# FFN 2 of a hybrid encoder layer: feature tiles 2 and 3 move from single units to a 2x2 pair, and the norms' small steps are reordered

## The chip, the cores and the metric

The kernel runs on one core of a Trainium2 chip. The metric is the device time of one execution in microseconds (us). The engines are named as in the profile: PE (TensorE, the matmuls; PEld are its weight loads), DVE (VectorE), ACT (ScalarE), POOL (GpSimd), SP (SyncE, which issues the loads).

## The reference

One layer on 512 tokens of width 1024 in float32: a half-step SwiGLU FFN, a mixer with two branches (a gated linear recurrence and a windowed attention), their gated sum through `w_o`, and a second half-step FFN. Each is wrapped in RMS norms.

```python
h = h + 0.5 * rms_norm(swiglu(rms_norm(h, ffn1_pre_g), ffn1_w1, ffn1_w3, ffn1_w2), ffn1_post_g)
u = rms_norm(h, mix_pre_g)
...
y_b = swa_sink_attention(q, k, v, attn_sinks, bias) @ w_attn_out
merged = g[:, :, 0] * y_a + g[:, :, 1] * y_b
h = h + rms_norm(merged @ w_o, mix_post_g)
f = swiglu(rms_norm(h, ffn2_pre_g), ffn2_w1, ffn2_w3, ffn2_w2)
h = h + 0.5 * rms_norm(f, ffn2_post_g)
```

`swiglu(x, w1, w3, w2)` is `(silu(x @ w1) * (x @ w3)) @ w2` with an inner width of 2816, which is 22 feature tiles of 128.

## The kernel before

**Number format.** Each float32 operand of a matmul is split in two: ACT copies it to a rounded `hi`, DVE subtracts to get `lo` (`split2`, L186; for weights `split_to`, L146 to L160). A product is three matmuls: hi by hi, lo by hi, hi by lo. The normalized and transposed input of an FFN lies in `uT` (hi and lo, 8 k-tiles of 128 x 512 tokens).

**A unit** (`unit`, `mm_feat`, L194 to L211) is one feature tile of one weight: 8 k-tiles x 3 = 24 matmuls of 128 x 512. In mid-stream it calls `point` twice; `later(n, fn)` (L170) puts a step on a hand-planned list that falls due n points on. So the order of work on ACT, DVE and POOL beside the matmuls is written out by hand.

**A pair** (`Pairs`, L460 to L582) takes two feature tiles of one weight as a 2x2 block product with seven multiplications in place of eight. A job is seven products (`mm_s`, L447) of 4 k-tiles x 3 matmuls of 128 x 256. Its right-hand operands are three quarters of `uT` (`b11`, `b21`, `b22`) and T1 to T4, sums of the quarters (`sums`, L729), which have to be split as well (`to_slots`, L738; `to_uT`, into `uT` itself, L743). Its left-hand operands are quarters of the two raw weight tiles and their sums S1 to S4: `prep(m, 0)` adds them on POOL (L500 to L503), `prep(m, 1)` to `prep(m, 4)` split the raw tile, S1/S2, S3/S4 and the last quarter on ACT and DVE (L191, L192). `run` makes the next job's `prep` 1 to 4 and the sums of the one behind it beside each job. The product with T4 of a job is issued behind the next job's second product (`last`). ACT evicts the first product of a job at L532.

**FFN 2 before** is tiles 0 and 1 as units inside w_o's function, tiles 2 and 3 as four units (`swiglu_units("w1b", "w3b", 2, NC2, hid)`, NC2 = 4), then nine pairs (18 jobs), then the product with w2.

**Around it.** The eight w_attn_out units (`for i in range(8)` behind `mg_out`, L1120 to L1135) come first; then w_o in `tok_gemm` (L314 to L401): for the first two k-tiles all token blocks, then four token blocks one after the other, each followed by its norms, with PE turning the result by transposes (L294). At its end the `first` list of four weights (tiles 0 and 1 of w1 and w3) is multiplied with token columns 0 to 255, and after the last transposes with columns 256 to 511. The T sums and the first job's weights are made beside these last halves and beside tiles 2 and 3.

**The norms.** `post_norm` (L253 to L268) takes two halves of 512 columns from PSUM: ACT squares and sums one (`junk`), DVE multiplies it with the gain (`fg`). `rstd2` (L227 to L235) then makes one over the root in five steps: `b` (DVE) from the first half's sum, the root `r` (ACT) from the second half's sum with `b` as bias, `v`, `e` and `r2` (DVE). DVE adds the result to `h` (L266). `norms` (L270 to L286) follows with the next norm's squares and products (`hg`, L278) and a second `rstd2`. The last token block of FFN 2 calls `post_norm` with three parts and stores each.

**Memory and queues.** All large tiles share 42 slots of 128 x 1024 float32 (NSLOT); a load is issued when a slot is free and in the fixed sequence `order`, on SP's queue. Matmul results use 8 PSUM banks. Each engine works in order.

Of the kernel before, what the change touches and what calls it, by code (L numbers as in the profile page):

```python
# [51 lines left out]
def hybrid_layer(ctx: ExitStack, tc: tile.TileContext, a: dict, out: bass.AP):  # L52
# [171 lines left out]

    NEWT = -0.5 * D**0.5

    def rstd2(ss):  # L227

        b, v, r, e, r2 = (small(1, x) for x in ("b", "v", "r", "e", "r2"))
        dve.tensor_scalar(out=b, in0=ss[:, 0:1], scalar1=D * EPS, scalar2=None, op0=ALU.add)  # L230
        act.activation(r, ss[:, 1:2], AF.Abs_reciprocal_sqrt, bias=b)
        dve.tensor_scalar(out=v, in0=ss[:, 1:2], scalar1=b, scalar2=None, op0=ALU.add)
        dve.tensor_scalar(out=e, in0=r, scalar1=v, scalar2=r, op0=ALU.mult, op1=ALU.mult)
        dve.tensor_scalar(out=r2, in0=e, scalar1=-3.0, scalar2=r, op0=ALU.add, op1=ALU.mult)
        return r2  # L235

    def rstd4(s4):

# [11 lines left out]
        pool.dma_start(out=t, in_=bass.AP(tensor=src.tensor, offset=src.offset, ap=[[0, P], [1, D]]))  # L250
        return t

    def post_norm(acc, t, gpost, scale, dst, after=None, parts=()):  # L253

        ss = small(2, "ss")
        fg = slot([P, D], name="fg")
        junk = slot([P, D], name="junk")
        cs = [slice(n * 512, (n + 1) * 512) for n in range(2)]
        for n, c in enumerate(cs):
            act.activation(junk[:, c], acc[n], AF.Square, accum_out=ss[:, n : n + 1])  # L260
            dve.scalar_tensor_tensor(out=fg[:, c], in0=acc[n], scalar=scale * NEWT, in1=gpost[:, c], op0=ALU.mult, op1=ALU.mult)
        r = rstd2(ss)
        if len(parts) > 2:
            cs = parts
        for n, c in enumerate(cs):
            dve.scalar_tensor_tensor(out=dst[:, c], in0=fg[:, c], scalar=r, in1=h[t][:, c], op0=ALU.mult, op1=ALU.add)  # L266
            if after:
                after(n, c)  # L268

    def norms(acc, t, gpost, scale, gpre, spill):  # L270

        hg = slot([P, D], name="hg")
        junk = slot([P, D], name="junk")
        ss = small(2, "ss")

        def half(n, c):
            act.activation(junk[:, c], h[t][:, c], AF.Square, accum_out=ss[:, n : n + 1])
            dve.scalar_tensor_tensor(out=hg[:, c], in0=h[t][:, c], scalar=NEWT, in1=gpre[:, c], op0=ALU.mult, op1=ALU.mult)  # L278

        post_norm(acc, t, gpost, scale, h[t], half)  # L280
        if spill:
            sp.dma_start(out=h_scr[t], in_=h.pop(t))
        r = rstd2(ss)
        dve.tensor_scalar(out=hg[:, :512], in0=hg[:, :512], scalar1=r, scalar2=None, op0=ALU.mult)
        act.activation(hg[:, 512:], hg[:, 512:], AF.Copy, scale=r)
        return hg  # L286
# [24 lines left out]
            act.activation(xf[half, t // 2][:, :, (t % 2) * P : (t % 2 + 1) * P], v, AF.Copy)  # L311


    def tok_gemm(nm, xs, n, R, gpost_name, scale, gpre_name, first, x_to=None, xf=None, spill=False):  # L314

# [37 lines left out]
        for t in range(NT):  # L355
            for ns in ((0,), (1,)):
                for k in range(F, n):
                    mm_tok(accs(t), xs[k], t, w[k], k == 0, k == n - 1, ns)
            if not gpre_name:
                o = slot([P, D], name="o")  # L360

                def store(nn, c, t=t, o=o):
                    sp.dma_start(out=out[t * P : (t + 1) * P, c], in_=o[:, c])

                last = (slice(0, 512), slice(512, 768), slice(768, D)) if t == NT - 1 else ()
                post_norm(acc[t], t, gpost, scale, o, store, last)
                continue
            if t == NT - 1:
                break
            if t >= 1:  # L370
                trs[t - 1] = transpose_mm(us[t - 1])
            if t == NT - 2:

                transpose_out(trs[t - 1], t - 1)
            us[t] = norms(acc[t], t, gpost, scale, gpre, spill)
            if t == NT - 2 and xf:
                transpose_xf(trs[t - 1], t - 1, xf)
            elif t == 1:
                transpose_out(trs[t - 1], t - 1, xf)
# [4 lines left out]
        for i, key in enumerate(first):  # L384
            ws.append(get(*key, ahead=len(first) - 1 - i, rawahead=2))
            bs.append(bank("f"))
            if i == len(first) - 1:
                trs[t] = transpose_mm(us[t])
                transpose_out(trs[t], t)
                if xf:  # L390
                    transpose_xf(trs[t - 1], t - 1, xf)
                    transpose_xf(trs[t], t, xf)
            mm_feat(bs[i], ws[i], 0, 256)
            if i == 0:
                trs[t - 1] = transpose_mm(us[t - 1])
                us[t] = norms(acc[t], t, gpost, scale, gpre, spill)
                transpose_out(trs[t - 1], t - 1)
# [62 lines left out]
    class Pairs:  # L460
# [13 lines left out]
        def prep(self, m, i, eng=None):  # L474
# [41 lines left out]
        def run(self, tail, hooks={}):
# [604 lines left out]
    def mg_out(i, ps):  # L1121
# [5 lines left out]
        dve.scalar_tensor_tensor(out=m[:, 1, :], in0=t, scalar=0.5, in1=f32(m[:, 0, :]), op0=ALU.mult, op1=ALU.subtract)  # L1127
        mg.append(m)

    for i in range(8):  # L1130
        if i:
            w = get("wao", i)
        ps = bank("f")
        mm_feat(ps, w, xh=xh, xl=xl)
        later(1, lambda i=i, ps=ps: mg_out(i, ps))  # L1135
    del xh, xl, OH, OL, KS, QS, BT
    h_load([h_scr[t] for t in range(NT)])
    xf = {(hh, th): slot([P, 4, 256], name="xf") for hh in range(2) for th in range(2)}
    bs = tok_gemm("wo", mg, KT, RO, "mix_post_g", 1.0, "ffn2_pre_g", [("w1b", 0), ("w3b", 0), ("w1b", 1), ("w3b", 1)], xf=xf)


    hid = Hidden()
    X2, tn = {"b11": uview(0, 0), "b21": uview(1, 0), "b22": uview(1, 1)}, []
    later(1, lambda: hid.f.append(silu_mul(bs[0], bs[1])))
    later(2, lambda: hid.f.append(silu_mul(bs[2], bs[3])))
    later(1, lambda: tn.extend(sums(xf)))
    later(2, lambda: xf.clear())
    for i in range(3):
        later(2 + i, lambda i=i: X2.update({f"t{i + 1}": to_slots(tn[i])}))
    pairs_b = Pairs("w1b", "w3b", NC2, X2, hid)  # L1150
    end = 2 * 2 * (NC2 - 2)
    for i, at_ in enumerate((end - 7, end - 4, end - 3, end - 2, end - 1)):
        later(at_, lambda i=i: pairs_b.prep(0, i))
    later(end, lambda: pairs_b.prep(1, 0))
    swiglu_units("w1b", "w3b", 2, NC2, hid)
    point(True)
    X2["t4"] = to_uT(tn[3], 0, 1)
    tn.clear()
    pairs_b.run(w2_ahead)
    X2 = pairs_b = None  # L1160
    tok_gemm("w2b", hid, FT, RF, "ffn2_post_g", 0.5, None, [], hid.to)

# [12 lines left out]
RO = 6  # L1175

NC1 = 6
NC2 = 4


# [52 lines left out]
```

## Time and profile before

| what | value |
|---|---|
| median of 3 runs | 1137.44 us (1137.4 to 1137.97) |
| profiled execution | 1138.07 us |
| its span in the profile | 1136.3 us |
| granted TensorE clock | 0.999 |
| w_attn_out units, first to last matmul | 692.2 to 735.4 us of the span |
| w_o with its norms | 735.5 to 781.4 us |
| tiles 0 and 1, then tiles 2 and 3 as units | 781.4 to 806.1, 806.1 to 827.9 us |
| nine pairs | from 827.9 us |

Instruction rows in what follows give the start in us, the duration, the engine, the line, the operation, output <- inputs, shapes, how many are merged, and in brackets how long the engine was idle before and what released it. Rows of grouped instructions give busy us, mean ns of one, and the idle time before them with its releasers.

### The profile page before, as it was taken

Reading aid. Unit: us, or ns where it says so; the run is one execution under the profiler, and the core shown is the slowest. Engines: PE = TensorE matmul, PEld = TensorE weight load, DVE = VectorE, ACT = ScalarE, POOL = GpSimd, SP = SyncE. Lnnn points to the kernel's source line nnn. Section 1 sums busy time; section 2 is a strip of 40 time slices with the busy share of each in tenths; the row PEclk is TensorE's granted clock in tenths of the full one; section 3 lists DMA queues with packets and bytes.
Section 4 is the critical chain, followed back from the end, with each engine's and each line's share of the span. In section 5 each row is a group of like instructions: output and inputs, shape, how many; then the busy total and the mean of one; then the engine's idle time right before and its main releaser. Section 6 shows DMA issues by size and latency. Waiting matters only on the chain.

```text
span 1136.3 us, 17136 instructions
## 1 busy us (share of the span) xinstructions
PE 1127.3 (99%) x6691; PEld 1001.7 (88%) x6691; DVE 779.9 (69%) x1170; ACT 579.1 (51%) x1028; POOL 340.5 (30%) x257
## 2 busy tenths in 40 slices
PE   9999999999999999999999999999999999999997
PEld 7889999988889987888888888889899999998886
DVE  5987879885436747695778854667968677985313
ACT  6445555574325359944656652356445555574211
POOL 0148677500000000001555640000655567700000
PEclk9999999999999999999999999999999999999999
DMA  9953223264313312234132333532123332265101
GB/s 337 164 132 112 92 95 112 80 218 152 107 56 136 143 56 61 71 101 140 56 92 76 94 103 103 170 125 93 45 87 112 112 106 82 93 196 175 39 19 55
DMA packets 36944, 124.93 MB, mean 110 GB/s; under 512 B 4416, under 2 KB 6208, under 8 KB 36864
## 3 DMA queue, kind: packets, MB, share of 16 engines
q1 hardware_dynamic: 34272, 115.15, 30.6%
q0 software_dynamic: 2448, 8.43, 3.9%
q8 instruction: 52, 0.85, 0.3%
q10 hardware_dynamic: 144, 0.26, 0.1%
q14 instruction: 28, 0.23, 0.1%
HBM read 116.50 MB, written 7.33 MB: 109 GB/s over the span
## 4 chain that ended last, share of the span: by engine, by line
PE 93%; DVE 3%; ACT 2%; issue 1%; DMA 0%; DVEq 0%; ACTq 0%
PE f L202 11%; PE f L201 11%; PE f L203 11%; PE c L457 10%; PE c L456 10%; PE c L455 10%; PE acc L219 8%; PE acc L221 8%; PE acc L220 8%; PE pt L1048 1%; PE s L1012 1%; PE s L1011 1%; PE tr L294 1%; PE o L1064 1%; PE o L1065 1%
## 5 line engine op out<-in xcount | busy, mean ns | idle before, releaser
L201 PE MATMUL f<-uT,whi 128*128 128x512 f32 (+1 forms) x536 | 196.6, 367 | 0.0
L202 PE MATMUL f<-uT,wlo 128*128 128x512 f32 (+1 forms) x536 | 195.4, 365 | 0.3 <-DVE wlo L157 0.3
L203 PE MATMUL f<-uT,whi 128*128 128x512 f32 (+1 forms) x536 | 195.1, 364 | 0.0
L219 PE MATMUL acc<-whi,hT 128*128 128x512 f32 x352 | 137.1, 390 | 0.0
L220 PE MATMUL acc<-wlo,hT 128*128 128x512 f32 x352 | 137.0, 389 | 0.0
L221 PE MATMUL acc<-whi,hT 128*128 128x512 f32 x352 | 136.9, 389 | 0.0
L201 PEld LDWEIGHTS f<-uT,whi 128*128 128x128 f32 x536 | 101.2, 189 | 17.0 <-issue 1.4
L202 PEld LDWEIGHTS f<-uT,wlo 128*128 128x128 f32 x536 | 101.2, 189 | 16.9 <-DVE wlo L157 1.6
L192 DVE TENSOR_TENSOR wlo<-S,whi 128x1024 fp32r<-128x1024 f32 x68 | 112.7, 1657 | 4.1 <-ACT whi L191 3.8
L456 PE MATMUL c<-Xh,wlo 128*128 128x256 f32 x408 | 115.5, 283 | 0.0
L457 PE MATMUL c<-Xl,whi 128*128 128x256 f32 x408 | 115.5, 283 | 0.0
L457 PE MATMUL c<-uT,whi 128*128 128x256 f32 x408 | 115.5, 283 | 0.0
L456 PE MATMUL c<-uT,wlo 128*128 128x256 f32 x408 | 115.5, 283 | 0.0
L455 PE MATMUL c<-Xh,whi 128*128 128x256 f32 x408 | 115.5, 283 | 0.0
L455 PE MATMUL c<-uT,whi 128*128 128x256 f32 x408 | 115.5, 283 | 0.0
L203 PEld LDWEIGHTS f<-uT,whi 128*128 128x128 f32 x536 | 101.1, 189 | 16.0
L1032 POOL TENSOR_SCALAR P<-P,d 128x256 f32<-128x256 f32 (+1 forms) x64 | 62.9, 998 | 55.0 <-DVE d L1030 42.0
L455 PEld LDWEIGHTS c<-Xh,whi 128*128 128x128 f32 x408 | 78.3, 192 | 0.0
L456 PEld LDWEIGHTS c<-uT,wlo 128*128 128x128 f32 x408 | 78.3, 192 | 0.0
L456 PEld LDWEIGHTS c<-Xh,wlo 128*128 128x128 f32 x408 | 78.3, 192 | 0.0
L455 PEld LDWEIGHTS c<-uT,whi 128*128 128x128 f32 x408 | 78.3, 192 | 0.0
L457 PEld LDWEIGHTS c<-Xl,whi 128*128 128x128 f32 x408 | 78.3, 192 | 0.0
(308 smaller groups left out, 2679.8 us busy)
## 6 DMA issues: line engine op xcount, KB each, us to landing
raw_w2a<-in_w2a_dram SPq DMA_DIRECT2D x22, 512.0 KB, 4.0
raw_w1b<-in_w1b_dram SPq DMA_DIRECT2D x22, 512.0 KB, 4.2
raw_w3b<-in_w3b_dram SPq DMA_DIRECT2D x22, 512.0 KB, 3.9
raw_w2b<-in_w2b_dram SPq DMA_DIRECT2D x22, 512.0 KB, 4.3
raw_w3a<-in_w3a_dram SPq DMA_DIRECT2D x21, 512.0 KB, 4.4
raw_w1a<-in_w1a_dram SPq DMA_DIRECT2D x20, 512.0 KB, 4.4
raw_wg<-in_wg_dram SPq DMA_DIRECT2D x16, 512.0 KB, 3.7
raw_xr<-in_xr_dram SPq DMA_DIRECT2D x8, 512.0 KB, 4.5
```

Of the source, the lines that this page charges most:

```text
L192: dve.tensor_tensor(out=lo, in0=src, in1=f32(hi), op=ALU.subtract)
L201: pe.matmul(ps[:, c0:c1], wh[:, s], h_, start=k == 0, stop=False)
L202: pe.matmul(ps[:, c0:c1], wl[:, s], h_, start=False, stop=False)
L203: pe.matmul(ps[:, c0:c1], wh[:, s], l_, start=False, stop=k == KT - 1)
L219: pe.matmul(acc[n], x[:, 0, c], wh[:, s], start=first, stop=False)
L220: pe.matmul(acc[n], x[:, 0, c], wl[:, s], start=False, stop=False)
L221: pe.matmul(acc[n], x[:, 1, c], wh[:, s], start=False, stop=last)
L294: pe.transpose(ps[:, k * P : (k + 1) * P], hg[:, kk * P : (kk + 1) * P], ident)
L455: pe.matmul(ps, wh[:, s], xh, start=first, stop=False, skip_group_check=True)
L456: pe.matmul(ps, wl[:, s], xh, start=False, stop=False, skip_group_check=True)
L457: pe.matmul(ps, wh[:, s], xl, start=False, stop=k == 3, skip_group_check=True)
L1032: pool.tensor_scalar(out=pt[:, x, b0:256], in0=pt[:, x, b0:256], scalar1=d[:, x : x + 1], scalar2=None, op0=ALU.mult)
```

## The change

NC2 becomes 2: tiles 2 and 3 of FFN 2 become a pair, so that there are ten pairs (20 jobs) and no unit behind w_o's function. The first job's two raw weights are loaded behind w_attn_out's, and its five `prep` steps stand on the due list of the w_attn_out units. A new function `operands` is called in `tok_gemm` behind the last transposes: it makes T1 and T2 with their splits, T3 on POOL, and the second job's sums on POOL. T4, T3's split and the SwiGLU of tiles 0 and 1 follow `tok_gemm`; T4's split is a hook in the first job. In the norms `rstd2` becomes three calls: `first` (`b`), `root` (`r`, `v`) and `value` (`e`, `r2`), which stand where their inputs are ready. A tiny Silu ahead of T1 loads ACT's table. `scale * NEWT` is now multiplied by the callers, with the same value.

```diff
--- before.py
+++ after.py
@@ -224,15 +224,22 @@
 
     NEWT = -0.5 * D**0.5
 
-    def rstd2(ss):
-        b, v, r, e, r2 = (small(1, x) for x in ("b", "v", "r", "e", "r2"))
-        dve.tensor_scalar(out=b, in0=ss[:, 0:1], scalar1=D * EPS, scalar2=None, op0=ALU.add)
-        act.activation(r, ss[:, 1:2], AF.Abs_reciprocal_sqrt, bias=b)
-        dve.tensor_scalar(out=v, in0=ss[:, 1:2], scalar1=b, scalar2=None, op0=ALU.add)
-        dve.tensor_scalar(out=e, in0=r, scalar1=v, scalar2=r, op0=ALU.mult, op1=ALU.mult)
-        dve.tensor_scalar(out=r2, in0=e, scalar1=-3.0, scalar2=r, op0=ALU.add, op1=ALU.mult)
-        return r2
+    class Rstd2:
+        def first(self, ss):
+            self.b, self.v, self.r, self.e, self.r2 = (small(1, x) for x in ("b", "v", "r", "e", "r2"))
+            dve.tensor_scalar(out=self.b, in0=ss[:, 0:1], scalar1=D * EPS, scalar2=None, op0=ALU.add)
+        def root(self, ss):
+            act.activation(self.r, ss[:, 1:2], AF.Abs_reciprocal_sqrt, bias=self.b)
+            dve.tensor_scalar(out=self.v, in0=ss[:, 1:2], scalar1=self.b, scalar2=None, op0=ALU.add)
+        def value(self):
+            dve.tensor_scalar(out=self.e, in0=self.r, scalar1=self.v, scalar2=self.r, op0=ALU.mult, op1=ALU.mult)
+            dve.tensor_scalar(out=self.r2, in0=self.e, scalar1=-3.0, scalar2=self.r, op0=ALU.add, op1=ALU.mult)
+            return self.r2
 
     def rstd4(s4):
 
@@ -250,18 +257,23 @@
         pool.dma_start(out=t, in_=bass.AP(tensor=src.tensor, offset=src.offset, ap=[[0, P], [1, D]]))
         return t
 
-    def post_norm(acc, t, gpost, scale, dst, after=None, parts=()):
+    def post_norm(acc, t, gpost, scale, dst, after=None, last=False):
 
         ss = small(2, "ss")
         fg = slot([P, D], name="fg")
         junk = slot([P, D], name="junk")
         cs = [slice(n * 512, (n + 1) * 512) for n in range(2)]
+        rs = Rstd2()
         for n, c in enumerate(cs):
             act.activation(junk[:, c], acc[n], AF.Square, accum_out=ss[:, n : n + 1])
-            dve.scalar_tensor_tensor(out=fg[:, c], in0=acc[n], scalar=scale * NEWT, in1=gpost[:, c], op0=ALU.mult, op1=ALU.mult)
-        r = rstd2(ss)
-        if len(parts) > 2:
-            cs = parts
+            if n:
+                rs.root(ss)
+            dve.scalar_tensor_tensor(out=fg[:, c], in0=acc[n], scalar=scale, in1=gpost[:, c], op0=ALU.mult, op1=ALU.mult)
+            if not n:
+                rs.first(ss)
+        r = rs.value()
+        if last:
+            cs = [slice(0, 512), slice(512, 768), slice(768, D)]
         for n, c in enumerate(cs):
             dve.scalar_tensor_tensor(out=dst[:, c], in0=fg[:, c], scalar=r, in1=h[t][:, c], op0=ALU.mult, op1=ALU.add)
             if after:
@@ -272,15 +284,19 @@
         hg = slot([P, D], name="hg")
         junk = slot([P, D], name="junk")
         ss = small(2, "ss")
+        rs = Rstd2()
 
         def half(n, c):
             act.activation(junk[:, c], h[t][:, c], AF.Square, accum_out=ss[:, n : n + 1])
+            if n:
+                rs.first(ss)
             dve.scalar_tensor_tensor(out=hg[:, c], in0=h[t][:, c], scalar=NEWT, in1=gpre[:, c], op0=ALU.mult, op1=ALU.mult)
 
-        post_norm(acc, t, gpost, scale, h[t], half)
+        post_norm(acc, t, gpost, scale * NEWT, h[t], half)
         if spill:
             sp.dma_start(out=h_scr[t], in_=h.pop(t))
-        r = rstd2(ss)
+        rs.root(ss)
+        r = rs.value()
         dve.tensor_scalar(out=hg[:, :512], in0=hg[:, :512], scalar1=r, scalar2=None, op0=ALU.mult)
         act.activation(hg[:, 512:], hg[:, 512:], AF.Copy, scale=r)
         return hg
@@ -311,7 +327,8 @@
             act.activation(xf[half, t // 2][:, :, (t % 2) * P : (t % 2 + 1) * P], v, AF.Copy)
 
 
-    def tok_gemm(nm, xs, n, R, gpost_name, scale, gpre_name, first, x_to=None, xf=None, spill=False):
+    def tok_gemm(nm, xs, n, R, gpost_name, scale, gpre_name, first, x_to=None, xf=None, spill=False, then=None):
 
 
 
@@ -362,8 +379,7 @@
                 def store(nn, c, t=t, o=o):
                     sp.dma_start(out=out[t * P : (t + 1) * P, c], in_=o[:, c])
 
-                last = (slice(0, 512), slice(512, 768), slice(768, D)) if t == NT - 1 else ()
-                post_norm(acc[t], t, gpost, scale, o, store, last)
+                post_norm(acc[t], t, gpost, scale * NEWT, o, store, t == NT - 1)
                 continue
             if t == NT - 1:
                 break
@@ -390,6 +406,8 @@
                 if xf:
                     transpose_xf(trs[t - 1], t - 1, xf)
                     transpose_xf(trs[t], t, xf)
+                if then:
+                    then()
             mm_feat(bs[i], ws[i], 0, 256)
             if i == 0:
                 trs[t - 1] = transpose_mm(us[t - 1])
@@ -511,6 +529,7 @@
                 t = slot([P, 2, QH], F32R, name="w22")
                 split2(t[:, 0, :], t[:, 1, :], a22)
                 W["a22"] = t[:, 0, :], t[:, 1, :]
+            if all((m, x) in self.ready for x in range(5)):
                 del W["r"], W["s"]
 
         def run(self, tail, hooks={}):
@@ -1127,6 +1146,14 @@
         dve.scalar_tensor_tensor(out=m[:, 1, :], in0=t, scalar=0.5, in1=f32(m[:, 0, :]), op0=ALU.mult, op1=ALU.subtract)
         mg.append(m)
 
+    hid, tn = Hidden(), []
+    X2 = {"b11": uview(0, 0), "b21": uview(1, 0), "b22": uview(1, 1)}
+    pairs_b = Pairs("w1b", "w3b", NC2, X2, hid)
+    dma_one(pairs_b.k0)
+    dma_one(pairs_b.k0 + 1)
+    for i, at_ in enumerate((2, 5, 7, 9, 11)):
+        later(at_, lambda i=i: pairs_b.prep(0, i))
     for i in range(8):
         if i:
             w = get("wao", i)
@@ -1136,27 +1163,31 @@
     del xh, xl, OH, OL, KS, QS, BT
     h_load([h_scr[t] for t in range(NT)])
     xf = {(hh, th): slot([P, 4, 256], name="xf") for hh in range(2) for th in range(2)}
-    bs = tok_gemm("wo", mg, KT, RO, "mix_post_g", 1.0, "ffn2_pre_g", [("w1b", 0), ("w3b", 0), ("w1b", 1), ("w3b", 1)], xf=xf)
-    hid = Hidden()
-    X2, tn = {"b11": uview(0, 0), "b21": uview(1, 0), "b22": uview(1, 1)}, []
-    later(1, lambda: hid.f.append(silu_mul(bs[0], bs[1])))
-    later(2, lambda: hid.f.append(silu_mul(bs[2], bs[3])))
-    later(1, lambda: tn.extend(sums(xf)))
-    later(2, lambda: xf.clear())
-    for i in range(3):
-        later(2 + i, lambda i=i: X2.update({f"t{i + 1}": to_slots(tn[i])}))
-    pairs_b = Pairs("w1b", "w3b", NC2, X2, hid)
-    end = 2 * 2 * (NC2 - 2)
-    for i, at_ in enumerate((end - 7, end - 4, end - 3, end - 2, end - 1)):
-        later(at_, lambda i=i: pairs_b.prep(0, i))
-    later(end, lambda: pairs_b.prep(1, 0))
-    swiglu_units("w1b", "w3b", 2, NC2, hid)
-    point(True)
-    X2["t4"] = to_uT(tn[3], 0, 1)
-    tn.clear()
-    pairs_b.run(w2_ahead)
+    def operands():
+        act.activation(small(4, "tiny")[:, 0:1], vec[:, 0:1], AF.Silu)
+        t = [slot([P, 4, 256], name="T") for _ in range(4)]
+        tn.extend(t)
+        dve.tensor_tensor(out=t[0], in0=xf[0, 1], in1=xf[0, 0], op=ALU.subtract)
+        X2["t1"] = to_slots(t[0])
+        dve.tensor_tensor(out=t[1], in0=xf[1, 1], in1=t[0], op=ALU.subtract)
+        X2["t2"] = to_slots(t[1])
+        pool.tensor_tensor(out=t[2], in0=xf[1, 1], in1=xf[0, 1], op=ALU.subtract)
+        pairs_b.prep(1, 0)
+    bs = tok_gemm(
+        "wo", mg, KT, RO, "mix_post_g", 1.0, "ffn2_pre_g",
+        [("w1b", 0), ("w3b", 0), ("w1b", 1), ("w3b", 1)], xf=xf, then=operands)
+    dve.tensor_tensor(out=tn[3], in0=xf[1, 0], in1=tn[1], op=ALU.subtract)
+    xf.clear()
+    hid.f.append(silu_mul(bs[0], bs[1]))
+    X2["t3"] = to_slots(tn[2])
+    hid.f.append(silu_mul(bs[2], bs[3]))
+    del bs
+    late = {(0, 1): [lambda: X2.update(t4=to_uT(tn[3], 0, 1)), tn.clear]}
+    pairs_b.prep(1, 1)
+    pairs_b.run(w2_ahead, late)
     X2 = pairs_b = None
     tok_gemm("w2b", hid, FT, RF, "ffn2_post_g", 0.5, None, [], hid.to)
 
@@ -1175,7 +1206,7 @@
 RO = 6
 
 NC1 = 6
-NC2 = 4
+NC2 = 2
 
 
 # ---- launch: one core; inputs laid out for contiguous loads ----
```

## The prediction

> **What bounds the kernel now.** I read the page first (engine shares, then the chain that ended last), then the busy time of each engine by stretches of the span, then the instructions of the stretches that the change touches.
>
> ```profile
> span 1136.3 us, 17136 instructions
> PE 1127.3 (99%) x6691; PEld 1001.7 (88%) x6691; DVE 779.9 (69%) x1170; ACT 579.1 (51%) x1028; POOL 340.5 (30%) x257
> PE 93%; DVE 3%; ACT 2%; issue 1%; DMA 0%; DVEq 0%; ACTq 0%
> ```
>
> TensorE (PE) is busy for 99% of the span and carries 93% of the chain. So only three things can move the time: the number and shape of its matmuls, a wait that opens or closes in its stream, and the few microseconds behind its last matmul. The next view gives, for four stretches, the microseconds and then the busy time of PE, PEld (weight loads), DVE, ACT and POOL: the w_attn_out units, w_o with its norms, the four units that the change removes, and 16 jobs of the pair stage.
>
> ```profile
> 692.20:735.40 43.20, 43.20 (x192) 35.77 (x191) 24.85 (x30) 13.67 (x17) 0.00 (x0) 1.00 0.42 135
> 735.50:781.40 45.90, 45.83 (x211) 37.82 (x210) 32.33 (x61) 24.29 (x49) 1.13 (x2) 1.00 0.30 95
> 806.14:827.92 21.78, 21.78 (x98) 18.03 (x97) 16.33 (x12) 8.40 (x10) 10.32 (x6) 1.00 0.30 97
> 838.20:999.48 161.28, 161.28 (x1346) 161.28 (x1345) 129.06 (x138) 87.10 (x153) 102.14 (x59) 1.00 0.30 99
> ```
>
> PE has no hole in any of them but a small one in w_o, at a granted clock of 1.00.
>
> **Part 1: tiles 2 and 3 as a pair.** Before, these tiles are four units of 24 matmuls with 512 columns (tiles 0 and 1, which w_o's function computes in two halves, stay). So 96 wide matmuls go, and two jobs of 7 x 4 x 3 = 84 matmuls with 256 columns come.
>
> ```profile
> 806.14 0.40 PE L201 MATMUL f<-uT,whi 128*128 128x512 f32 x1
> ...
> 827.93 0.28 PE L455 MATMUL c<-uT,whi 128*128 128x256 f32 x1
> 838.20 0.38 ACT L532 ACTIVATE ct<-c 128x256 f32<-128x256 f32 x1 [0.54 <-PE c L457]
> ...
> 999.48 0.38 ACT L532 ACTIVATE ct<-c 128x256 f32<-128x256 f32 x1 [0.54 <-PE c L457]
> L532 ACT ACTIVATE ct<-c 128x256 f32<-128x256 f32 x17 | 6.5, 383 | 9.1 <-PE c L457 9.1
> ```
>
> From the units' first matmul to the first one of a job pass 827.93 - 806.14 = 21.79 us: 0.227 us a matmul. L532 evicts each job's first product; 17 of them are 16 periods, (999.48 - 838.20) / 16 = 10.08 us a job: 0.120 us a matmul. The term is 2 x 10.08 - 21.79 = **-1.63 us**, if PE starves nowhere.
>
> The Trainium skill speaks against it. Its page "TensorE: Matmul & The Clock Gate", section "Back-to-back issue gap", says that in a stream the spacing is set by weight load and matmul together, about 81 ns at 128 columns and 131 ns at 512. Interpolated to 98 ns at 256 (an estimate from that page), 96 x 131 - 168 x 98 ns is a loss of 3.9 us, not a gain. The rows disagree (0.227 and 0.120), and they decide.
>
> **Part 2: the norms' small steps.** The operations stay; their order changes. `b` needs only the first half's sum of squares and now stands ahead of the second half's product on DVE; ACT's root follows its own second square at once. In most norms PE has other work meanwhile. The hole in w_o is at the first token block:
>
> ```profile
> 762.72 0.39 PE L221 MATMUL acc<-whi,mg 128*128 128x512 f32 x1
> 763.18 1.09 PE L294 MATMUL tr<-ident,hg 128*128 128x128 f32 x8
> 764.03 0.49 PE L219 MATMUL acc<-whi,mg 128*128 128x512 f32 x1
> ...
> 763.18 0.42 PEld L294 LDWEIGHTS tr<-ident,hg 128*128 128x128 f32 x4 [0.49 <-DVE hg L284]
> ...
> 784.26 1.04 PE L294 MATMUL tr<-ident,hg 128*128 128x128 f32 x8
> 785.05 0.36 PE L201 MATMUL f<-uT,whi 128*128 128x256 f32 x1
> ```
>
> The transposes start 0.46 us behind the matmul ahead of them where a pitch is 0.227, and hold PE for 0.85 us where the unstalled ones hold it for 0.79. That is 0.235 + 0.06, about 0.29 us, and it goes if `hg` comes 0.24 us or more earlier. Its chain:
>
> ```profile
> 755.48 0.19 ACT L260 ACTIVATION_READ_ACCUMULATOR junk<-acc 128x1 f32 x1
> 755.71 0.69 DVE L261 SCALAR_TENSOR_TENSOR fg<-acc,bc_mix_post_g 128x512 f32<-128x512 f32 x1 [3.39 <-ACT junk L260]
> ...
> 756.53 1.28 ACT L231 ACT_TABLE_LOAD   x1 [0.86 <-DVE b L230]
> ```
>
> The table load for the root starts 0.86 us behind the sum because it waits for `b`, which waits for the product. After the change it starts at about 755.68, so everything behind it comes some 0.85 us earlier: 0.6 us more than needed. Term **-0.29 us**, bounds 0 and -0.29.
>
> Behind the last matmul nothing hides these steps:
>
> ```profile
> 1129.76 0.19 ACT L260 ACTIVATION_READ_ACCUMULATOR junk<-acc 128x1 f32 x1
> ...
> 1129.98 0.69 DVE L261 SCALAR_TENSOR_TENSOR fg<-acc,bc_ffn_post_g 128x512 f32<-128x512 f32 x1 [4.07 <-ACT junk L260]
> 1130.59 0.14 DVE L230 TENSOR_SCALAR b<-ss 128x1 f32<-128x1 f32 x1
> 1130.77 0.21 DVE L232 TENSOR_SCALAR v<-ss,b 128x1 f32<-128x1 f32 x1
> 1130.83 0.29 ACT L231 ACTIVATE r<-ss,b 128x1 f32<-128x1 f32 x1 [0.88 <-DVE b L230]
> 1131.16 0.27 DVE L233 TENSOR_SCALAR e<-r,v 128x1 f32<-128x1 f32 x1 [0.17 <-ACT r L231]
> ```
>
> Now ACT takes the root at 1129.98 and is done at 1130.27; DVE does `v` at 1129.98, the product 0.2 later and `e` 0.61 behind that (the product-to-`b` pitch): 1130.79 instead of 1131.16. Term **-0.37 us**, bounds 0 (the order is undone by a wait that I don't see) and -0.61 (all that `b` cost).
>
> **Part 3: what loses its cover.** Before, the 21.78 us of units hid 16.33 us of DVE, 8.40 of ACT and 10.32 of POOL: tile 0 and 1's SwiGLU, the sums T1 to T4 and their hi/lo splits, the first job's weights. Now job 0 begins at about 805.9, as soon as w_o's second halves end.
>
> Job 0's weights (four sums on POOL, four splits on ACT and DVE) move beside the w_attn_out units, where the second view shows POOL idle, ACT 13.67 and DVE 24.85 of 43.20 us busy. They fit: priced at nothing.
>
> Their raw tiles and results hold slots longer. So two raw weights of w_o's `first` list are issued later on SP, behind w_o's first 48 matmuls (about 746.3 us), and ACT's splits of them stand in ACT's queue ahead of the first norm's squares:
>
> ```profile
> 737.39 0.33 SPq L141 DMA_DIRECT2D raw_w1b<-in_w1b_dram  x1
> 744.13 0.33 SPq L141 DMA_DIRECT2D raw_w3b<-in_w3b_dram  x1
> ...
> 746.43 1.06 ACT L156 ACTIVATE whi<-raw_w1b 128x1024 fp32r<-128x1024 f32 x1 [1.81 <-DMA raw_w1b<-in_w1b_dram]
> 747.80 1.06 ACT L156 ACTIVATE whi<-raw_w3b 128x1024 fp32r<-128x1024 f32 x1 [0.32 <-DMA raw_w3b<-in_w3b_dram]
> ```
>
> From issue to the ACT instruction that it releases these took 3.7 and 9.0 us. At 3.7 to 5 us the late ones land by 751.5, and their two splits end by 753.6; the squares of the first norm ended at 755.67 (the accumulator's row above). I price it at nothing; at 9.0 us the splits end at 757.4, and the chain is 2.5 us late: bound +1.6 us behind its 0.85 of advance.
>
> T1, T2 and the second job's sums follow w_o's last transposes, on DVE and POOL together. These two slow each other:
>
> ```profile
> 794.66 2.41 POOL L732 TENSOR_TENSOR T<-xf,xf 128x1024 f32<-128x1024 f32 x1 [57.28 <-ACT xf L311]
> 797.04 2.26 POOL L500 TENSOR_TENSOR S<-raw_w1b 128x512 f32<-128x512 f32 x1
> ...
> 795.56 2.60 DVE L157 TENSOR_TENSOR wlo<-raw_w1b,whi 128x1024 fp32r<-128x1024 f32 x1 [1.87 <-ACT whi L156]
> 798.08 2.31 DVE L157 TENSOR_TENSOR wlo<-raw_w3b,whi 128x1024 fp32r<-128x1024 f32 x1
> ...
> 807.14 1.23 DVE L735 TENSOR_TENSOR T<-xf,T 128x1024 f32<-128x1024 f32 x1
> ...
> 826.90 1.29 POOL L501 TENSOR_TENSOR S<-S,raw_w1b 128x512 f32<-128x512 f32 x1
> ```
>
> Alone a DVE sum or split of 128x1024 takes 1.23 us and a POOL sum of 128x512 1.29; side by side they take 2.3 to 2.6, as if one at a time. From 795 us on, DVE has nine such operations up to the third split of job 1's weights (T1, its split, T2, its split, T4, T3's and T4's splits, the raw and the S12 split of job 1), and POOL has T3 (2.41) and eight sums. At about 1.1 us each in turn that is 9 x 1.13 + 2.3 + 8 x 1.1 = 21 us: S12's split ends at about 815.5. Job 1 starts at 805.9 + 8.6 (its last product belongs behind the next job's second) and needs it in its second product at 816.0; T1 (798.5 against 807.3), T2 (804 against 808.8), T3 (809 against 813.2) and T4 (813 against 817.4) have more. So **nothing** is added, with 0.5 us in hand; with POOL at 1.29 it ends at 817, a stall of 1.0 us, and below nothing there is no gain since PE has no hole here. The Trainium skill's page "SBUF — State Buffer", section "SBUF: two separate sides", calls this shared port pair an exclusive lock held for the whole instruction; by the rows (2.60 against 1.23) the trace agrees.
>
> **Sum:** -1.63 - 0.29 - 0.37 = **-2.29 us**. The profiled execution is 1138.07 us (span 1136.3 and 1.77 around it) and would be 1135.78; it lies 0.63 above the median of the runs, 1137.44, which so becomes 1135.15, or **1135.2 us**.
>
> **The rivals.**
>
> *Job 1 waits for its weights* (the 1.0 us above, at most 1.7 if no two operations of DVE and POOL overlap at 1.23 and 1.29 x 9): -2.29 + 1.0 = -1.3, 1136.2 us. For it: the margin is an estimate of 0.5 us in a stretch of 21. Against: PSUM readers (0.68 us) and ACT's share aren't slowed, and POOL's later sums could wait behind DVE's without harm.
>
> *The first norm comes late*, because ACT holds two splits whose loads land after 754: -2.29 + 0.29 + 1.0 = -1.0, 1136.4 us. For it 9.0 us of the one row, against it 3.7 of the other.
>
> *The moved steps don't pay* (the order changes, the waits stay): -1.63, 1135.8 us.
>
> *Short matmuls run at their weight loads' pace.* PEld is busy for all 161.28 us of the pair stage. If the two new jobs' matmuls came at 0.150 instead of 0.120 us, 168 x 0.030 = 5.0 more: +2.7, 1140.2 us; the turning point is (21.79 + 0.66) / 168 = 0.134. The skill's rule, named above, points this way with 3.9. Against: 16 x 84 matmuls of the very same shape at 0.120.
>
> *Slower: the pair stage lives on a head start that is gone.* If DVE and POOL work strictly in turn, a job needs three splits of 1.23, one of half the size (0.6), four sums of 1.29 and about 1.0 of DVE's products with two SBUF inputs: 10.45 us where PE needs 10.08. Before, 21.8 us of units would have covered 18 x 0.37 = 6.7 of lag unseen; without them 19 jobs pay 0.37 each: +7.0, in sum +4.7, 1142.1 us. It decides from 10.20 us a job (19 x 0.12 = 2.3). Against it speaks that POOL waits for free buffers in these very jobs:
>
> ```profile
> L500 POOL TENSOR_TENSOR S<-raw_w1b 128x512 f32<-128x512 f32 x7 | 12.1, 1729 | 27.9 <-DVE w L192 6.0 <-DVE cc L566 5.4 <-DVE wlo L192 5.1
> L500 POOL TENSOR_TENSOR S<-raw_w3b 128x512 f32<-128x512 f32 x7 | 10.0, 1432 | 22.2 <-PE c L456 6.5 <-PE c L457 6.1 <-DVE wlo L192 4.1
> ```
>
> 27.9 + 22.2 = 50.1 us idle in 161.28, some 3 us a job: the stage isn't behind.
>
> **How the numbers follow.** Chances: the forecast 0.55, job 1's wait 0.15, the late norm 0.08, moved steps without effect 0.08, the weight loads' pace 0.02, the lost head start 0.12. About 0.2%, 2.27 us, is what a measurement of this kernel can tell from no change; the bounds are 1135.17 and 1139.71, and the forecast of 1135.15 lies on the first. Its bounds reach from 1134.9 (the tail at -0.61) to 1135.6, plus 0.3 of scatter as in the runs before. I give 0.34 of its 0.55 to faster, since only the port and the loads, which have cases of their own, take from it, and 0.21 to within; with 0.15 + 0.08 + 0.08 within is 0.52, and slower is 0.02 + 0.12 = 0.14. The range is 1134.6 to 1137.2: from the forecast's lower end with its scatter to the late norm and job 1's wait at their dearer ends (1.6 and 1.7 us) with 0.3 of scatter or, less likely, some of both; outside lie the slower cases, 0.14, and little else.
>
> **What would show it.** Right: job period 10.08 from the first pair on, no PE gap between w_o's second halves and the pairs, transposes 0.23 us behind the matmul ahead in w_o's first norm, and 0.37 us less from the last square to `e`. Wrong: a PE wait on a DVE `wlo` near 816 us (first rival), ACT's `whi` splits of w_o's last list behind 754 us (second), the table load still behind the product (third), evictions of a job's first product more than 10.08 us apart in the first jobs alone (fourth) or all along with POOL never idle (fifth). A wait that no row here shows, such as a slot that comes free later than I traced, would make the whole wrong.

## The result, and the profile after

The changed kernel takes **1135.38 us** (median of 22 runs, 1134.98 to 1137.82), the kernel before 1137.50 in the same comparison (22 runs, 1137.31 to 1138.41). The ratio is 0.9981 with a 95% interval of 0.9975 to 0.9987: 2.1 us less (1.5 to 2.8). The profiled execution fell from 1138.07 to 1135.67 us. The forecast was 2.29 less, 1135.2 us. The page's first lines after, and the window of busy times of 16 jobs (PE, PEld, DVE, ACT, POOL) with the w_o window ahead of it:

```profile
span 1133.8 us, 17339 instructions
PE 1125.3 (99%) x6763; PEld 1003.5 (89%) x6763; DVE 790.1 (70%) x1181; ACT 585.2 (52%) x1042; POOL 353.8 (31%) x265
```

```profile
735.50:781.40 45.90, 45.90 (x214) 38.25 (x213) 32.39 (x61) 24.90 (x49) 1.13 (x2) 1.00 0.24 79
...
836.13:997.41 161.28, 161.28 (x1346) 161.28 (x1345) 131.74 (x139) 87.18 (x152) 100.18 (x59) 1.00 0.29 99
```

72 more matmuls, 2.0 us less of PE, and now no hole in w_o either: 45.90 of 45.90 us.

**PE term.** The first matmul of the pairs follows the units' halves without a gap, and L551 (L532 before) evicts each job's first product:

```profile
805.57 0.28 PE L203 MATMUL f<-uT,whi 128*128 128x256 f32 x1
805.69 0.28 PE L473 MATMUL c<-uT,whi 128*128 128x256 f32 x1
```

```profile
836.13 0.39 ACT L551 ACTIVATE ct<-c 128x256 f32<-128x256 f32 x1 [0.54 <-PE c L475]
...
997.41 0.38 ACT L551 ACTIVATE ct<-c 128x256 f32<-128x256 f32 x1 [0.54 <-PE c L475]
```

17 evictions, so (997.41 - 836.13) / 16 = 10.08 us a job, as before. From the end of the halves to the last job's eviction it is 997.41 - 805.69 = 191.72 us, where the kernel before took 999.48 - 806.14 = 193.34: -1.62 us (forecast -1.63).

**Norm term.** The transposes of w_o's first norm, and the table load ahead of its root:

```profile
762.61 0.39 PE L221 MATMUL acc<-whi,mg 128*128 128x512 f32 x1
762.84 1.03 PE L310 MATMUL tr<-ident,hg 128*128 128x128 f32 x8
763.63 0.48 PE L219 MATMUL acc<-whi,mg 128*128 128x512 f32 x1
```

```profile
755.37 0.19 ACT L268 ACTIVATION_READ_ACCUMULATOR junk<-acc 128x1 f32 x1
755.58 1.28 ACT L236 ACT_TABLE_LOAD   x1
```

They come 0.23 us behind the matmul ahead and hold PE for 0.79: the hole is gone (0.235 + 0.06, forecast -0.29). The load starts 0.02 us behind the sum where it had waited 0.86.

**End term.** Behind the last matmul:

```profile
1127.69 0.19 ACT L268 ACTIVATION_READ_ACCUMULATOR junk<-acc 128x1 f32 x1
1127.92 0.29 ACT L236 ACTIVATE r<-ss,b 128x1 f32<-128x1 f32 x1
1127.92 0.21 DVE L237 TENSOR_SCALAR v<-ss,b 128x1 f32<-128x1 f32 x1 [4.01 <-ACT junk L268]
1128.05 0.68 DVE L271 SCALAR_TENSOR_TENSOR fg<-acc,bc_ffn_post_g 128x512 f32<-128x512 f32 x1
1128.65 0.27 DVE L240 TENSOR_SCALAR e<-r,v 128x1 f32<-128x1 f32 x1
```

From the accumulator to `e` it is 1128.65 - 1127.69 = 0.96 us, before 1131.16 - 1129.76 = 1.40: -0.44 (forecast -0.37; the product followed `v` by 0.13, not 0.2).

The three are -2.36 us; the profiled executions differ by 2.40, the medians by 2.12, whose interval holds both. Single profiles also start differently: the first 60 matmuls, which wait for the first loads, came anywhere from 0.1 us later to 0.8 us earlier than in the trace of before, in the kernels traced here. So traces are compared below from there on. Counted so, the changed kernel's trace is 2.36 us shorter too: 1.91 at PE and 0.45 behind it.

### The profile page after: what moved, and what is told of

Its sections match the earlier page's. It is cut to its first block, busy times and chain, and to the rows that moved or that the text cites. A ratio compares the mean times of both kernels' runs of the same rounds, so it can differ in the third digit from the quotient of the medians.

```text
span 1133.8 us, 17339 instructions
## 1 busy us (share of the span) xinstructions
PE 1125.3 (99%) x6763; PEld 1003.5 (89%) x6763; DVE 790.1 (70%) x1181; ACT 585.2 (52%) x1042; POOL 353.8 (31%) x265
## 4 chain that ended last, share of the span: by engine, by line
PE 93%; DVE 3%; ACT 2%; issue 1%; DMA 0%; SPq 0%; DVEq 0%
PE c L475 11%; PE c L474 11%; PE c L473 11%; PE f L202 10%; PE f L201 10%; PE f L203 10%; PE acc L220 8%; PE acc L221 8%; PE acc L219 8%; PE pt L1067 1%; PE s L1031 1%; PE s L1030 1%; PE tr L310 1%; PE o L1083 1%; PE o L1084 1%
## 5 line engine op out<-in xcount | busy, mean ns | idle before, releaser
L201 PE MATMUL f<-uT,whi 128*128 128x512 f32 (+1 forms) x504 | 184.2, 365 | 0.0
L202 PE MATMUL f<-uT,wlo 128*128 128x512 f32 (+1 forms) x504 | 183.0, 363 | 0.4 <-DVE wlo L157 0.3
L203 PE MATMUL f<-uT,whi 128*128 128x512 f32 (+1 forms) x504 | 182.6, 362 | 0.0
L474 PE MATMUL c<-Xh,wlo 128*128 128x256 f32 x432 | 122.3, 283 | 0.0
L475 PE MATMUL c<-Xl,whi 128*128 128x256 f32 x432 | 122.3, 283 | 0.0
L473 PE MATMUL c<-uT,whi 128*128 128x256 f32 x432 | 122.3, 283 | 0.0
L474 PE MATMUL c<-uT,wlo 128*128 128x256 f32 x432 | 122.3, 283 | 0.0
L475 PE MATMUL c<-uT,whi 128*128 128x256 f32 x432 | 122.3, 283 | 0.0
L473 PE MATMUL c<-Xh,whi 128*128 128x256 f32 x432 | 122.3, 283 | 0.0
L202 PEld LDWEIGHTS f<-uT,wlo 128*128 128x128 f32 x504 | 95.2, 189 | 15.8 <-DVE wlo L157 1.6
L201 PEld LDWEIGHTS f<-uT,whi 128*128 128x128 f32 x504 | 95.1, 189 | 15.8 <-issue 1.4
L203 PEld LDWEIGHTS f<-uT,whi 128*128 128x128 f32 x504 | 95.1, 189 | 14.8
L473 PEld LDWEIGHTS c<-uT,whi 128*128 128x128 f32 x432 | 82.9, 192 | 0.0
L475 PEld LDWEIGHTS c<-uT,whi 128*128 128x128 f32 x432 | 82.9, 192 | 0.0
```

What stands on the lines that cost most here:

```text
L201: pe.matmul(ps[:, c0:c1], wh[:, s], h_, start=k == 0, stop=False)
L202: pe.matmul(ps[:, c0:c1], wl[:, s], h_, start=False, stop=False)
L203: pe.matmul(ps[:, c0:c1], wh[:, s], l_, start=False, stop=k == KT - 1)
L473: pe.matmul(ps, wh[:, s], xh, start=first, stop=False, skip_group_check=True)
L474: pe.matmul(ps, wl[:, s], xh, start=False, stop=False, skip_group_check=True)
L475: pe.matmul(ps, wh[:, s], xl, start=False, stop=k == 3, skip_group_check=True)
```

## The experiments

Ratios are to the kernel before; its median beside these runs was 1137.5 to 1137.6 us.

**1. The norms' steps alone** (the kernel before with `Rstd2` and the new `post_norm` and `norms`).

```diff
+        rs = Rstd2()
         for n, c in enumerate(cs):
             act.activation(junk[:, c], acc[n], AF.Square, accum_out=ss[:, n : n + 1])
+            if n:
+                rs.root(ss)
...
+            if not n:
+                rs.first(ss)
-        r = rstd2(ss)
+        r = rs.value()
```

> The kernel before with only the norms' small steps moved up, tiles 2 and 3 still as units. Theory (the three terms add up and don't touch each other): the 0.29 us hole at w_o's first transposes closes and the end behind the last square shortens by about 0.4 us, so some 0.7 us below the kernel before, ratio 0.9994, about 1136.8 us. Rival (the pair brings nothing, the whole gain is the norms'): 2.1 us, ratio 0.998, 1135.4 us. Rival (the hole closed because weight loads and their splits moved, which only the pair brings): the hole of 0.24 us ahead of the transposes stays, and only 0.4 us at the end is gained.

Measured: 1136.95 us, ratio 0.9995 (0.9986 to 1.0003), 0.6 us less. In its trace the hole in w_o is closed without the pair, and the trace from the 60th matmul on is 0.77 us shorter: 0.32 at PE and 0.45 behind it. The interval includes no change, so the trace carries this one.

**2. The pair alone** (the changed kernel with the old `rstd2`, `post_norm` and `norms`).

```diff
-            if n:
-                rs.root(ss)
...
-            if not n:
-                rs.first(ss)
-        r = rs.value()
+        r = rstd2(ss)
```

> The changed kernel with the norms' small steps in their old order: only the pair and the moves that feed it. Theory: 2 x 10.08 - 21.79 = -1.63 us and nothing else, ratio 0.9986, about 1135.9 us, with the 0.29 us hole in w_o back. The old order starts w_o's last norm some 0.5 us later; as T1 has over 9 us in hand that costs nothing. Rival (the pair brings nothing): ratio 1.000, 1137.5 us. Rival (the pair brings all): ratio 0.998, 1135.4.

Measured: 1136.60 us, ratio 0.9991 (0.9983 to 1.0000), 0.9 to 1.0 us less where 1.63 was expected (in its trace, from the 60th matmul on, PE is done 1.1 us earlier). The two parts alone make 1.6, both together 2.1. The intervals are wider than this difference; that the parts aren't independent is shown by the trace. The hole in w_o's first norm is back, as expected, and there is a new one ahead of the last block's transposes, which wasn't expected; the DVE row is the third block's first product:

```profile
790.21 0.28 PE L203 MATMUL f<-uT,whi 128*128 128x256 f32 x1
790.78 1.06 PE L294 MATMUL tr<-ident,hg 128*128 128x128 f32 x8 [0.29 <-DVE hg L284]
```

```profile
775.15 1.29 DVE L261 SCALAR_TENSOR_TENSOR fg<-acc,bc_mix_post_g 128x512 f32<-128x512 f32 x2 [0.35 <-ACT junk L260]
```

0.57 - 0.12 = 0.45 us of PE, a wait for `hg`. In the changed kernel the same transposes follow at 0.12 us. The chain of norms runs some 0.7 us later than in the kernel before, about half of it by the wait for ACT in front of the third block. So the moved steps also cover a delay that the pair's moves bring.

**3. Slots held, no pair** (the kernel before with four idle slots held from the fifth w_attn_out unit to w_o's last transposes).

```diff
+        if i >= 4 and len(hold) < 4:
+            for _ in range(2):
+                hold.append(slot([P, D], name="hold"))
+                pool.memset(hold[-1][:, :1], 0.0)
...
```

> The kernel before (units for tiles 2 and 3, norms in their old order) with four empty slots held from the fifth w_attn_out unit to w_o's last transposes, as the first job's weights hold slots in the changed kernel. Two weights of w_o's last list are then loaded behind w_o's matmuls. Theory (the pair alone lost 0.5 us of its 1.63 since the held slots make the norms of w_o late, and the hole of 0.45 us that the pair-only kernel shows ahead of the last transposes is this): a hole of 0.2 to 0.5 us ahead of the last transposes, 1137.7 to 1138.0 us, ratio 1.0002 to 1.0004. Rival (the slots don't matter, the hole came from the moved preps or operands): no hole there, 1137.5 us.

Measured: 1137.68 us, ratio 1.0001 (0.9992 to 1.0009), and no hole ahead of the last transposes. Late loads alone (ACT's last split at 750.24, against 747.80 before) cost nothing: the theory as I put it failed. Four held slots also shift the norms' tiles in the ring of slots otherwise than the moved steps do, so this run says nothing about that cause.

**4. One slot less for each norm** (the pair alone, with both squares of a block written into one slot).

```diff
         hg = slot([P, D], name="hg")
-        junk = slot([P, D], name="junk")
...
-            act.activation(junk[:, c], h[t][:, c], AF.Square, accum_out=ss[:, n : n + 1])
+            act.activation(self_junk[0][:, c], h[t][:, c], AF.Square, accum_out=ss[:, n : n + 1])
```

> The pair-only kernel (norms in their old order) with one thing more: in the norms of w_o both squares of a block throw their elements into one slot in place of two, so that each norm takes one slot less and its first product no longer waits for the second half's square. Theory (the half microsecond that the pair-only kernel lost is a wait of the norms' new tiles for recently used slots: 0.35 us at the third block's first product): the hole of 0.45 us ahead of the last transposes goes, or falls below 0.1, and the pair's full 1.63 us show: 1135.9 us, ratio 0.9986. Rival (the lateness comes from elsewhere, the loads or ACT's splits ahead of the first square): the hole stays, 1136.6 us.

Measured: 1140.14 us, ratio 1.0020 (1.0011 to 1.0029): 3.5 us *slower* than the pair alone. Its profiled execution is one of the shorter ones, 1138.77 us, 2.4 above that of the pair alone. The third block's first product in it:

```profile
777.40 1.29 DVE L263 SCALAR_TENSOR_TENSOR fg<-acc,bc_mix_post_g 128x512 f32<-128x512 f32 x2 [2.72 <-PE acc L220]
```

It waits 2.72 us for a matmul of w_o. By that releaser, its slot had held the lo half of a weight of w_o that PE still read. Two holes of 0.71 and 2.03 us open ahead of the next transposes, where the pair alone had one of 0.45; that is the 2.3 us by which its trace is longer. So the expected result was wrong, and the run shows that a norm's tile can be held up by what last read its slot. That the pair-only kernel's 0.35 us is a small case of the same isn't shown: which read made it stays open, and experiment 3 shows only that later loads alone don't make the hole.

**5. T1 to T4 where they had been** (behind the SwiGLU of tiles 0 and 1).

```diff
-        [("w1b", 0), ("w3b", 0), ("w1b", 1), ("w3b", 1)], xf=xf, then=operands)
+        [("w1b", 0), ("w3b", 0), ("w1b", 1), ("w3b", 1)], xf=xf)
...
+    hid.f.append(silu_mul(bs[0], bs[1]))
+    hid.f.append(silu_mul(bs[2], bs[3]))
+    operands()
...
```

> The changed kernel with T1 to T4 and their splits behind the SwiGLU of tiles 0 and 1 on ACT and DVE (the order that the kernel before had) and not behind the last transposes. Theory (the gain hangs on cover: the operands must be made beside w_o's second halves): DVE starts T1 at about 806.5 us, job 0's second product waits for T1's lo by about 3 us and its third for T2's by about 2 more: +5 us against the changed kernel, 4 to 7, so about 1140.4 us, ratio to the kernel before about 1.0025. Rival (DVE and ACT have room enough, the place doesn't matter): no change, 1135.4 us.

Measured: 1142.71 us, ratio 1.0048 (1.0033 to 1.0064), 7.3 us above the changed kernel, just over the 4 to 7 expected. PE waits for T1's halves and then, by the last row, for ACT's eviction of the job's first product (L551):

```profile
808.35 0.39 PE L473 MATMUL c<-Xh,whi 128*128 128x256 f32 x1 [1.64 <-ACT Xh L191]
...
809.61 0.38 PE L475 MATMUL c<-Xl,whi 128*128 128x256 f32 x1 [0.76 <-DVE Xl L192]
...
810.78 0.30 PE L475 MATMUL c<-Xl,whi 128*128 128x256 f32 x1
813.99 0.58 PE L473 MATMUL c<-Xh,whi 128*128 128x256 f32 x1 [2.91 <-ACT ct L551]
```

By the starts these are 1.8, 0.9 and 3.1 us: 5.8, near the 5 expected. But the last one, the longest, isn't the wait for T2 that was expected. T2's hi was done at 811.8 and its lo at 813.0. The third product adds to the bank that the eviction reads, and ahead of the eviction ACT splits T3 and the second job's raw weight:

```profile
811.68 1.04 ACT L191 ACTIVATE Xh<-T 128x1024 fp32r<-128x1024 f32 x1
812.63 1.04 ACT L191 ACTIVATE whi<-raw_w3b 128x1024 fp32r<-128x1024 f32 x1
813.58 0.36 ACT L551 ACTIVATE ct<-c 128x256 f32<-128x256 f32 x1
```

So operands without cover cost twice: PE waits for them, and their splits hold up the eviction behind them. Another 1.7 us follow the last wait; the windows' column behind POOL is the granted clock:

```profile
810.80:814.00 3.20, 0.29 (x4) 0.07 (x2) 2.19 (x2) 3.14 (x4) 3.12 (x2) 0.52 0.62 244
814.00:817.60 3.60, 3.60 (x17) 3.60 (x18) 3.60 (x3) 1.97 (x4) 3.52 (x3) 0.50 0.19 76
817.70:824.00 6.30, 6.30 (x54) 6.30 (x53) 6.30 (x6) 2.83 (x5) 2.79 (x3) 1.00 0.19 52
```

For 3.6 us behind the wait the granted clock is 0.50 and a matmul takes 0.21 us in place of 0.12. The last section comes back to it.

**6. Two more DVE operations ahead of job 1's splits** (T4's sum written three times).

```diff
     dve.tensor_tensor(out=tn[3], in0=xf[1, 0], in1=tn[1], op=ALU.subtract)
+    dve.tensor_tensor(out=tn[3], in0=xf[1, 0], in1=tn[1], op=ALU.subtract)
+    dve.tensor_tensor(out=tn[3], in0=xf[1, 0], in1=tn[1], op=ALU.subtract)
```

> The changed kernel with the subtraction that makes T4 written three times in place of once: two more DVE operations of 128x1024 in the stretch where DVE and POOL work in turn. Theory (first rival of the prediction, with the trace's margin: S12's split for job 1 ends at 814.0, needed at 815.9): two more turns of 2.3 us make it 818.6, so job 1's second product waits 1.6 to 2.7 us: 1137.0 to 1138.1 us. Rival (side by side they only share the port, DVE has idle time to give): under 0.3 us, 1135.4 to 1135.7 us. Rival (T4 or T3 is the tighter one): the wait stands ahead of a product with T3 or T4.

Measured: 1136.91 us, ratio 0.9993 (0.9984 to 1.0002), 1.5 above the changed kernel, just under the 1.6 to 2.7 expected. First DVE's S12 split and PE's use of it in the changed kernel, then both in this one:

```profile
811.68 2.32 DVE L192 TENSOR_TENSOR wlo<-S,whi 128x1024 fp32r<-128x1024 f32 x1
```

```profile
815.77 0.28 PE L473 MATMUL c<-Xh,whi 128*128 128x256 f32 x1
815.89 0.28 PE L474 MATMUL c<-Xh,wlo 128*128 128x256 f32 x1
```

```profile
815.64 1.21 DVE L192 TENSOR_TENSOR wlo<-S,whi 128x1024 fp32r<-128x1024 f32 x1
...
815.24 0.28 PE L473 MATMUL c<-Xh,whi 128*128 128x256 f32 x1
816.90 0.39 PE L474 MATMUL c<-Xh,wlo 128*128 128x256 f32 x1 [1.38 <-DVE wlo L192]
```

The wait stands exactly where the first rival put it, at the second product of job 1. In the changed kernel the split ends at 811.68 + 2.32 = 814.00 and is needed at 815.89, so 1.9 us are in hand. The two operations added 4.4 us (2.2 each). S12's split then took 1.21 us in place of 2.32, while POOL stood idle (814.6 to 816.9); with the 1.9 in hand, 1.5 reach PE.

**7 and 8. More POOL in every job** (the last sum written again, once or three times, in 17 jobs).

```diff
-                e.tensor_tensor(out=s34[:, :QH], in0=a11, in1=a21, op=ALU.subtract)
+                for _ in range(1 + 1 * (self.na == "w1b" and m >= 3)):
+                    e.tensor_tensor(out=s34[:, :QH], in0=a11, in1=a21, op=ALU.subtract)
```

> The changed kernel with one more POOL sum of 128x512 (the last one written twice) in each of the 17 jobs from the fourth on. Theory (the prediction's fifth rival is wrong: a job has some 3 us of POOL idle): the extra 1.3 to 1.8 us of POOL a job fit: no change, 1135.4 us, job period 10.08. Rival (DVE and POOL work in turn and a job needs about 10.45 us of them): every job is longer by 0.4 plus 1.3 us: about +29, 1164 us.

> The changed kernel with three more POOL sums of 128x512 in each of the 17 jobs from the fourth on. Theory (POOL has 3.1 us idle of 10.08 and each sum takes 1.3 alone or 1.73 on average beside DVE): 3.9 to 5.2 us more don't fit: a job takes 10.9 to 12.2 us, +14 to +36, 1149 to 1171 us. Rival (POOL's sums can always hide, since PE needs them only a job later): no change, 1135.4.

Measured: 1141.82 us with one more, ratio 1.0037 (1.0024 to 1.0051), +6.4 against the changed kernel; 1172.99 with three more, ratio 1.0313 (1.0297 to 1.0328), +37.6. Both theories missed the first: it isn't free, and it isn't 29. The second lies just above the 14 to 36 expected; its trace also has three stretches of 3.4 us at a granted clock of 0.50 (last section). The same stretch as in the changed kernel's window above, with one more sum a job:

```profile
836.13:997.41 161.28, 157.74 (x1301) 156.32 (x1301) 152.55 (x132) 84.06 (x147) 134.57 (x74) 1.00 0.28 95
```

15 more POOL operations take 134.57 - 100.18 = 34.4 us, 2.3 each, and DVE is busy 20.8 us longer with seven instructions fewer. A sum that takes 1.29 us alone costs 2.3 of POOL and 1.4 of DVE. DVE had 161.28 - 131.74 = 29.5 us idle in 16 jobs, 1.8 a job; now it has 0.5, and PE waits in some jobs (3.5 us in this stretch). All these waits are for DVE; the row gives the total of the whole execution, how often, and the longest:

```profile
PE c L474 <- DVE wlo L192: 3.8, 6, 1.2
```

**9. The same exchange in FFN 1** (`NC1 = 4`: tiles 4 and 5 as a pair).

```diff
-NC1 = 6
+NC1 = 4
```

> The changed kernel with the same exchange in FFN 1: tiles 4 and 5 as a pair too (NC1 = 4), with none of the operand steps moved ahead. Theory (a pair gains 1.63 us only where the operands are made under other matmuls; in FFN 1 DVE is busy for 45.6 of the 49 us ahead of the first pair): the 21.8 us of units taken away leave DVE about 11 us late with T1 to T4: PE waits there, +9 us in sum (5 to 14), 1144 us. Rival (PE's rows decide alone): -1.6, 1133.8 us.

Measured: one time of 1145.97 us, +10.6 against the changed kernel's median, within the 5 to 14 expected. The first job there waits for T1's hi and then, for longer, its lo:

```profile
53.95 0.38 PE L473 MATMUL c<-Xh,whi 128*128 128x256 f32 x1 [1.42 <-ACT Xh L191]
54.18 0.28 PE L474 MATMUL c<-Xh,wlo 128*128 128x256 f32 x1
59.80 0.58 PE L475 MATMUL c<-Xl,whi 128*128 128x256 f32 x1 [5.34 <-DVE Xl L192]
```

Again the granted clock is 0.50 for the 9 us behind that wait. If the pair saves the same 1.6 us at PE's rows, 12.2 are lost where the operands have no cover.

**10. A DVE order mended elsewhere** (the changed kernel, T4's sum in FFN 1 issued two points later).

```diff
     later(6, lambda: tn.extend(sums(xn)))
+    later(8, lambda: dve.tensor_tensor(out=tn[3], in0=xn[1, 0], in1=tn[1], op=ALU.subtract))
...
-        dve.tensor_tensor(out=t[3], in0=xf[1, 0], in1=t[1], op=ALU.subtract)
         return t
```

> The changed kernel with one DVE operation of FFN 1 (the sum T4, 1.2 us) issued two points later than T1 to T3, behind a unit's weight split that PE waits for at 57.2 us (0.46 us, and 0.11 behind it). Theory (as for w_o's norms: a small wait of PE on DVE goes when the DVE order gives the waited-for operation first): the 0.57 us hole goes, nothing else moves: 1134.8 us, ratio 0.9976. Rival (DVE is so dense in this stretch that the wait only moves to a later unit or to T4's use in the first pairs): 1135.4 us, and another hole of like size.

Measured: **1134.95 us**, ratio 0.9976 (0.9966 to 0.9986), the fastest version here. The changed kernel's matmul that waited, then the same place in this one:

```profile
57.22 0.39 PE L201 MATMUL f<-uT,whi 128*128 128x512 f32 x1
57.90 0.50 PE L202 MATMUL f<-uT,wlo 128*128 128x512 f32 x1 [0.30 <-DVE wlo L157]
58.24 0.39 PE L203 MATMUL f<-uT,whi 128*128 128x512 f32 x1
```

```profile
57.05 0.39 PE L201 MATMUL f<-uT,whi 128*128 128x512 f32 x1
57.28 0.39 PE L202 MATMUL f<-uT,wlo 128*128 128x512 f32 x1
57.51 0.39 PE L203 MATMUL f<-uT,whi 128*128 128x512 f32 x1
```

1.02 us become 0.46. Both kernels' intervals overlap, so that it beats the changed one rests on the trace: from the 60th matmul on, PE is done 0.59 us earlier.

## Why the prediction was right, step by step

- **Pair as rows of PE:** right. -1.62 measured for -1.63; the 10.08 us of a job held from the first pair on. The spacing of 98 ns that I interpolated from the Trainium skill's page "TensorE: Matmul & The Clock Gate", section "Back-to-back issue gap", and by which the pair would have lost, didn't hold for these matmuls: they came every 0.120 us.
- **Norms' steps:** right in mechanism and size for the two places that I priced (0.29 and 0.44 for 0.29 and 0.37). I missed a third use: without them the moves that feed the pair make the last norm late by 0.45 us of PE (experiment 2). The sum had no term for this delay. That the moved steps cover it wasn't forecast, and that it doesn't show in the changed kernel is luck: the norms alone came out as priced (experiment 1), the pair alone didn't.
- **The late loads:** right, nothing. The splits ended at 753.2, forecast 753.6. They cost the first norm nothing with the old norms either: in experiment 3 they ended at 751.3, in experiment 2 at 752.6, and its second square ended no later than before (within 0.03 us, counted from the 60th matmul).
- **Job 1's weights:** right that nothing waits, but not by my sum. 795 + 9 x 1.13 + 2.3 + 8 x 1.1 is 816.3, not 815.5: by its own terms the split was 0.3 us late, not 0.5 early (and with POOL at 1.29 it was 1.8 late, not 1.0). The margin was 1.9 us since the stretch began earlier and was shorter than I took: T1's sum began at 793.7, not 795, and three of DVE's turns took 1.6 to 1.7 us and two 1.2, not 2.3. So this "nothing" was partly luck. Experiment 6 puts the rival at its place, 1.5 us for 4.4 added.
- **The lost head start:** the stage isn't behind, as I said, but the evidence was read too generously. POOL's 3 us idle a job isn't room for 3 us of POOL: one more sum a job already costs 6.4 us in all (experiment 7), because each slows DVE as well. The scarce one is DVE, with 1.8 us a job.
- **Size against the bound:** 2.1 us less is 0.19%, just inside the 0.2% that I named as the bound; the forecast lay on it, and the interval (0.13 to 0.25%) reaches both sides of it, though not to no change.

## What to carry to other kernels

When PE is dense, price a rewrite by its rows on PE, and then ask only for each operand when it is ready and when it is needed: the same exchange gained 1.6 us with its operands made ahead, and without that ended 5 us above the kernel before in FFN 2, and 10.6 above the changed one in FFN 1. Where two engines slow each other, the idle time of one is no margin; add an operation and see what it takes from the other. Parts of a change needn't add up, since one can cover a delay that another brings: test them together and apart.

## What the runs showed of the hardware

A wait of PE can have an after-effect: the granted clock falls to 0.50, and in experiment 5 that cost 1.7 us more than the waits themselves. The length of one wait doesn't decide it. Behind waits of 1.5 us (experiment 6) and 1.8 us (experiment 5) the next matmuls ran at full pace. In experiment 5 the mean clock over the 3.2 us window of the last wait is 0.52, so the clock had fallen within 0.1 us of the start of that wait, behind waits of 1.8 and 0.9 us. In experiment 9 the mean of 0.62 in the first row below puts the fall 1.4 us into the window: a good 1 us into the wait of 5.5 us, with one of 1.6 us just ahead. The other rows are from experiment 8 with three more sums:

```profile
54.00:59.80 5.80, 0.46 (x3) 0.25 (x3) 5.73 (x6) 1.91 (x2) 0.00 (x0) 0.62 0.97 103
...
927.30:930.60 3.30, 1.39 (x12) 1.18 (x11) 3.30 (x4) 0.00 (x0) 3.14 (x3) 1.00 0.03 11
930.70:934.10 3.40, 3.40 (x18) 3.40 (x18) 3.40 (x4) 2.12 (x4) 3.32 (x3) 0.50 0.01 2
934.10:940.00 5.90, 5.90 (x51) 5.90 (x51) 5.26 (x4) 3.76 (x7) 5.74 (x4) 1.00 0.17 66
```

There PE waits 1.9 us and the clock is 0.50 for the next 3.4 us. This happens three times in that trace, whose longest wait is 2.1 us; behind five other waits of 1.9 to 2.1 us the clock stays at 1.00. What decides between them stays open. Experiment 4 has a sign of the same: of its eleven executions six took 1140.1 us or more at a mean granted clock of 0.997, five 1139.3 or less at 0.998 or 0.999. None of the six was traced.

The Trainium skill's page "TensorE: Matmul & The Clock Gate", section "What's actually happening", names an idle window of about 3.4 us for the drop and as much activity for the return. The drop doesn't agree with it: in experiment 8 it came behind a single wait of 1.9 us. The return agrees there (3.4 us) and nearly in experiment 5 (3.6 to 3.7 us behind the wait). In experiment 9 it took over 9 us, with a further wait of 0.8 us among them.
